# Image loads in fp32 through SyncE with casts on ScalarE, in a 3x3 convolution bound by its transfers

## Chip, cores, metric

One core of one Trainium2 chip. The metric is device time of one execution in microseconds (us). Runs are called slow when they are over 1.5% above the fastest of the same kernel; ratios and verdicts use the other, fast runs alone. Spans and windows come from one profiled execution of each kernel, a fast one in every case here. In profile lines PE is TensorE, PEld its weight loads, DVE VectorE, ACT ScalarE, POOL GpSimd and SP SyncE; a q behind a name is the engine's instruction queue, which waits and issues transfers. HBM is the memory that x and the output lie in, PSUM the one that TensorE's sums lie in. A transfer has landed when its completion is signalled.

## The reference

A 3x3 convolution, padding 1, stride 1, fp32 in and out: x is 16 x 64 x 64 x 64, the weight 128 x 64 x 3 x 3, the output 16 x 128 x 64 x 64.

```python
x_pad = np.pad(x, ((0, 0), (0, 0), (1, 1), (1, 1)), mode='constant')
for b, co, ci, kh, kw in all_indices:      # five nested loops
    output[b, co] += weight[co, ci, kh, kw] * x_pad[b, ci, kh:kh+h, kw:kw+w]
```

16.8 MB are read and 33.6 MB written.

## The kernel before

Two images of 64 channels fill the 128 partitions, so the batch is worked off in eight pairs; below, "image p" is the 2.1 MB load of pair p. Two output rows are computed together from three groups of fp16 matmuls: U from the sums of two neighbouring image rows (`ss`), A and B from the image itself (`xs`). ScalarE copies U out of PSUM, VectorE adds it to A and B. Each pair has four blocks of 30 matmuls. Loads 1 to 7 are issued by GpSimd and cast to fp16 on the way (casting loads); image 0 comes in fp32 in four pieces and is cast by ScalarE.

```python
    xpool = ctx.enter_context(tc.tile_pool(name="xpool", bufs=5))
    opool = ctx.enter_context(tc.tile_pool(name="opool", bufs=8))
    ...
    x0 = opool.tile([128, H, W], F32, tag="ot", name="x0")
    cuts = [(0, 18), (18, 34), (34, 50), (50, 64)]
    for lo, hi in cuts:
        nc.sync.dma_start(x0[:, lo:hi, :], x_rows[0:128, lo:hi, :])
    ...
    def load(p):
        xs[p] = xpool.tile([128, H, W], F16, tag="xs", name="xs")
        keep(nc.gpsimd.dma_start(xs[p], x_rows[128 * p : 128 * p + 128, :, :]))

    for p in range(1, 5):
        load(p)
    ...
    for p in range(NP):
        if p + 1 < NP:
            for lo in (0, 16):
                sums(nc.gpsimd, p + 1, xs[p + 1], lo, 16)
        if p > 0 and p + 4 < NP:
            load(p + 4)
        ...
        for blk in range(4):
            ...
            U = group([(G1, None)])          # 6 matmuls
            ...                              # two copies of U by ScalarE
            A = group([(G21, 1), (G0, -1)])  # 12 matmuls, then two adds
            Bt = group([(G01, 0), (G2, 2)])  # 12 matmuls, then two adds
            if blk in parts:
                ...                          # stores of the pair by SyncE
```

Of the kernel before, what the change touches and what calls it, by code (L numbers as in the profile page):

```python
# [8 lines left out]
F32 = mybir.dt.float32  # L9
F16 = mybir.dt.float16  # L10


@with_exitstack
def kernel(
    ctx: ExitStack,
    tc: tile.TileContext,
    x: bass.AP,
    weight: bass.AP,
    out: bass.AP,
):  # L20
    nc = tc.nc
    B, CI, H, W = x.shape
    CO = weight.shape[0]
    assert H == 64 and W == 64 and CI == 64 and CO == 128 and B % 2 == 0
    NP = B // 2
    RB = 8

    keep = tc.keep_in_program_order
    x_rows = x.rearrange("b c h w -> (b c) h w")
    out_rows = out.rearrange("b co h w -> b co h w")  # L30
    w_flat = weight.rearrange("co ci kh kw -> co (ci kh kw)")

    const = ctx.enter_context(tc.tile_pool(name="const", bufs=1))
    psum = ctx.enter_context(tc.tile_pool(name="psum", bufs=8, space=bass.MemoryType.PSUM))
    xpool = ctx.enter_context(tc.tile_pool(name="xpool", bufs=5))
    opool = ctx.enter_context(tc.tile_pool(name="opool", bufs=8))
    spool = ctx.enter_context(tc.tile_pool(name="spool", bufs=3))
    upool = ctx.enter_context(tc.tile_pool(name="upool", bufs=4))


    w_raw = const.tile([CO, CI * 9], F32)
    nc.sync.dma_start(w_raw, w_flat)  # L42
    x0 = opool.tile([128, H, W], F32, tag="ot", name="x0")
    cuts = [(0, 18), (18, 34), (34, 50), (50, 64)]
    for lo, hi in cuts:
        nc.sync.dma_start(x0[:, lo:hi, :], x_rows[0:128, lo:hi, :])  # L46
    ident = const.tile([128, 128], F16)
    make_identity(nc, ident)
    w16 = const.tile([CO, CI * 9], F16)
    keep(nc.gpsimd.tensor_copy(w16, w_raw))  # L50

    xs = {0: xpool.tile([128, H, W], F16, tag="xs", name="xs")}

    def load(p):
        xs[p] = xpool.tile([128, H, W], F16, tag="xs", name="xs")
        keep(nc.gpsimd.dma_start(xs[p], x_rows[128 * p : 128 * p + 128, :, :]))  # L56

    for p in range(1, 5):
        load(p)


    ss = {}

    def sums(eng, p, src, lo, n):
        if p not in ss:
            ss[p] = spool.tile([128, H // 2, W], F16, tag="ss", name="ss")
        v = src.rearrange("p (j i) c -> p j i c", i=2)
        keep(
            eng.tensor_add(  # L69
                ss[p][:, lo : lo + n, :], v[:, lo : lo + n, 0, :], v[:, lo : lo + n, 1, :]  # L70
            )
        )


    Wt = const.tile([128, 5, 3, CO], F16)
    G0, G21, G1, G01, G2 = range(5)

    def wrow(i):
        return Wt[:, i, :, :].rearrange("p t c -> p (t c)")

    wps = {}
    for kh in (1, 2, 0):
        wp = psum.tile([128, 512], F32, tag="acc", name="wp")
        for k in range(3):
            t = 3 * kh + k
            for q in (0, 64):
                nc.tensor.matmul(wp[q : q + 64, k * CO : k * CO + CO], w16[:, t::9], ident)  # L87
        wps[kh] = wp[:, 0 : 3 * CO]
    keep(nc.scalar.copy(wrow(G1), wps[1]))  # L89
    sums(nc.vector, 0, x0, 0, RB)  # L90
    keep(nc.vector.tensor_sub(wrow(G21), wps[2], wrow(G1)))  # L91
    keep(nc.vector.tensor_sub(wrow(G01), wps[0], wrow(G1)))  # L92
    for n, (lo, hi) in enumerate(cuts):
        keep(nc.scalar.copy(xs[0][:, lo:hi, :], x0[:, lo:hi, :]))  # L94
        if n == 0:
            keep(nc.scalar.copy(wrow(G0), wps[0]))  # L96
            keep(nc.scalar.copy(wrow(G2), wps[2]))  # L97
        if n < 3:
            sums(nc.vector, 0, x0, RB * (n + 1), RB)

    for p in range(NP):
        if p + 1 < NP:
            for lo in (0, 16):
                sums(nc.gpsimd, p + 1, xs[p + 1], lo, 16)
        if p > 0 and p + 4 < NP:
            load(p + 4)
        ots = [
            opool.tile([128, H // 2, 2, W], F32, tag="ot", name="ot") for _ in range(2)
        ]
        for blk in range(4):  # L110
            j0 = blk * RB

            def group(wi_rows):

                tiles = [
                    psum.tile([128, RB, W], F32, tag="acc", name="acc") for _ in range(2)
                ]
                n = 3 * len(wi_rows)
                i = 0
                for wi, off in wi_rows:  # L120
                    for kw in (1, 0, 2):
                        c_lo, c_hi = max(0, 1 - kw), min(W, W + 1 - kw)
                        for b2 in range(2):
                            p0 = 64 * b2
                            lo, hi = j0, j0 + RB
                            if off is None:
                                rhs = ss[p][p0 : p0 + 64, lo:hi, c_lo + kw - 1 : c_hi + kw - 1]
                            else:
                                while 2 * lo + off < 0:
                                    lo += 1  # L130
                                while 2 * (hi - 1) + off > H - 1:
                                    hi -= 1
                                first = 2 * lo + off
                                last = 2 * (hi - 1) + off
                                rhs = xs[p][
                                    p0 : p0 + 64,
                                    first : last + 1 : 2,
                                    c_lo + kw - 1 : c_hi + kw - 1,
                                ]
                            nc.tensor.matmul(  # L140
                                tiles[b2][:, lo - j0 : hi - j0, c_lo:c_hi],
                                Wt[p0 : p0 + 64, wi, kw, :],
                                rhs,
                                start=i == 0,
                                stop=i == n - 1,
                            )
                        i += 1
                return tiles

            U = group([(G1, None)])  # L150
            us = []
            for b2 in range(2):
                ut = upool.tile([128, RB, W], F32, tag="ut", name="ut")
                keep(nc.scalar.copy(ut, U[b2]))  # L154
                us.append(ut)
            A = group([(G21, 1), (G0, -1)])
            for b2 in range(2):
                nc.vector.tensor_add(ots[b2][:, j0 : j0 + RB, 0, :], A[b2], us[b2])  # L158
            Bt = group([(G01, 0), (G2, 2)])
            for b2 in range(2):  # L160
                nc.vector.tensor_add(ots[b2][:, j0 : j0 + RB, 1, :], Bt[b2], us[b2])  # L161
            parts = {3: (0, 64)} if p < NP - 1 else {1: (0, 32), 3: (32, 64)}
            if blk in parts:
                lo, hi = parts[blk]
                for b2 in range(2):
                    nc.sync.dma_start(
                        out_rows[2 * p + b2, :, lo:hi, :],
                        ots[b2].rearrange("p j i c -> p (j i) c")[:, lo:hi, :],
                    )


# [28 lines left out]
```

## Time and profile before

| | before |
|---|---|
| time, first runs (the last counts as slow) | 127.51, 128.91, 129.74 us |
| span of the profiled run | 125.7 us |
| busy: PE, VectorE, ScalarE, GpSimd | 107.0, 83.7, 40.8, 34.8 us |
| HBM traffic | 50.6 MB |

Busy time has to be read against what ends the kernel. The prediction quotes the rows that show both TensorE and the DMA engines full. What decides between them is the end of the chain of waits (columns: start, length, what), and whom SyncE, which issues the stores, waited for (total us, times, longest):

```profile
112.55 0.68 DVE ot L158
113.22 0.60 DVE ot L161
113.82 0.60 DVEq L195
```

```profile
SPq L166 <- DVE ot L161: 101.7, 17, 21.2
SPq L195 <- DMA out_dram<-ot: 8.9, 4, 2.4
```

The chain ends with VectorE 11 us before the span does. The closing lines of SyncE (L195) then wait 8.9 us for stores.

These are the groups that the change touches (busy us, mean ns of one; idle before it and its releaser):

```profile
L69 POOL TENSOR_TENSOR ss<-xs 128x1024 f16<-128x1024 f16 x14 | 29.5, 2125 | 23.1 <-DMA xs<-in_x_dram 9.3
L56 POOL DMA_DIRECT2D xs<-in_x_dram x7 | 4.0, 575 | 15.8 <-PE acc L140 15.8
```

### The profile page before, as it was taken

To read this page: it belongs to the slowest core of one execution; us is meant where nothing else is said; L and a number is where in the kernel's file an instruction comes from. 1 tells how busy PE (TensorE), PEld (TensorE's weight loads), DVE (VectorE), ACT (ScalarE), POOL (GpSimd) and SP (SyncE) were. 2 spreads that over 40 slices of the span, in tenths; PEclk is the share of its full clock that TensorE was granted. 3 is DMA by queue.
4 is the path that set the end of the run, shared out by engine and by line. 5 is a ranking of instruction groups with operands and counts; after the bars stand their busy time and mean duration, and the time that the engine had idled before them with its cause. 6 is when DMAs were issued, how large, how long until landed. Compare 5 with 4: busy or idle time off the path is not lost.

```text
span 125.7 us, 2408 instructions
## 1 busy us (share of the span) xinstructions
PE 107.0 (85%) x978; PEld 55.9 (44%) x978; DVE 83.7 (67%) x134; ACT 40.8 (32%) x72; POOL 34.8 (28%) x28
## 2 busy tenths in 40 slices
PE   0489799999999999999999999999999999990000
PEld 0334355555555555555555555555555555540000
DVE  0180798778877777877787778777877787773000
ACT  4283833333333333324333333333333333330000
POOL 2710297893029201930930093000000000000000
PEclk9999999999999999999999999999999999999755
DMA  4999999999999999999999999999999999999980
GB/s 130 325 353 216 224 214 222 211 182 331 326 305 362 315 315 323 422 321 326 307 409 443 433 427 438 417 422 433 427 433 438 417 422 433 427 417 422 422 370 34
DMA packets 4330, 43.43 MB, mean 345 GB/s; under 512 B 480, under 2 KB 480, under 8 KB 1120
## 3 DMA queue, kind: packets, MB, share of 16 engines
q1 hardware_dynamic: 3312, 35.95, 68.5%
q0 software_dynamic: 1008, 7.34, 28.5%
q8 instruction: 7, 0.11, 0.3%
q14 instruction: 3, 0.02, 0.0%
HBM read 17.07 MB, written 33.55 MB: 403 GB/s over the span
## 4 chain that ended last, share of the span: by engine, by line
PE 77%; DMA 8%; ACT 2%; SPq 1%; DVE 1%; issue 1%; DVEq 0%
PE acc L140 77%; DMA x<-in_x_dram 8%; SPq L46 1%; ACT ut L154 1%; ACT xs L94 1%; DVE ot L158 1%; DVEq L195 0%; DVE ot L161 0%; SPq L42 0%; DVEq L158 0%
## 5 line engine op out<-in xcount | busy, mean ns | idle before, releaser
L140 PE MATMUL acc<-xs,Wt 64*128 64x504 f16 (+3 forms) x768 | 95.1, 379 | 0.8 <-ACT ut L154 0.7
L140 PEld LDWEIGHTS <-Wt 64*128 64x128 f16 x960 | 54.8, 96 | 52.4 <-issue 5.1
L158 DVE TENSOR_TENSOR ot<-acc,ut 128x512 f32<-128x512 f32 x64 | 41.2, 686 | 21.2 <-PE acc L140 18.0
L154 ACT COPY ut<-acc 128x512 f32<-128x512 f32 x64 | 34.2, 589 | 64.1 <-issue 59.6
L161 DVE TENSOR_TENSOR ot<-acc,ut 128x512 f32<-128x512 f32 x64 | 41.1, 685 | 0.0
L69 POOL TENSOR_TENSOR ss<-xs 128x1024 f16<-128x1024 f16 x14 | 29.5, 2125 | 23.1 <-DMA xs<-in_x_dram 9.3
L140 PE MATMUL acc<-ss,Wt 64*128 64x504 f16 (+1 forms) x192 | 32.5, 384 | 0.9 <-DVE ss L69 0.9
L69 DVE TENSOR_TENSOR ss<-x 128x512 f16<-128x512 f32 x4 | 2.8, 690 | 9.6 <-DMA x<-in_x_dram 9.6
L56 POOL DMA_DIRECT2D xs<-in_x_dram x7 | 4.0, 575 | 15.8 <-PE acc L140 15.8
L87 PE MATMUL wp<-ident,w 128*64 128x128 f16 x18 | 1.3, 328 | 4.5 <-POOL w L50 4.5
L94 ACT CAST xs<-x 128x1024 f16<-128x1024 f32 (+2 forms) x4 | 4.1, 1052 | 2.4 <-DMA x<-in_x_dram 2.4
L87 PEld LDWEIGHTS <-w 128*64 128x64 f16 x18 | 1.1, 209 | 4.5 <-POOL w L50 4.5
L89 ACT ACT_TABLE_LOAD x1 | 1.3, 1283 | 0.7 <-PEq L184 0.7
L89 ACT CAST Wt<-wp 128x384 f16<-128x384 f32 x1 | 0.5, 480 | 3.1 <-PE wp L87 3.1
L50 POOL CAST w<-w_raw 128x576 f16<-128x576 f32 x1 | 0.7, 662 | 2.5 <-DMA w_raw<-in_weight_dram 2.5
L96 ACT CAST Wt<-wp 128x384 f16<-128x384 f32 x1 | 0.5, 479 | 0.5 <-DVE Wt L92 0.5
L91 DVE TENSOR_TENSOR Wt<-wp,Wt 128x384 f16<-128x384 f32 x1 | 0.6, 550 | 0.0
L92 DVE TENSOR_TENSOR Wt<-wp,Wt 128x384 f16<-128x384 f32 x1 | 0.5, 548 | 0.0
L97 ACT CAST Wt<-wp 128x384 f16<-128x384 f32 x1 | 0.5, 485 | 0.0
masks.py:199 POOL TENSOR_SCALAR_AFFINE_SELECT ident<-ident 128x128 f16<-128x128 f16 x1 | 0.3, 292 | 0.1
masks.py:197 POOL MEMSET ident<- 128x128 f16 x1 | 0.2, 204 | 0.3 <-POOLq L184 0.3
L184 POOL MEMSET const-float32-0.0<- 128x1 f32 x1 | 0.1, 98 | 0.2 <-issue 0.2
(3 smaller groups left out, 0.3 us busy)
## 6 DMA issues: line engine op xcount, KB each, us to landing
out_dram<-ot SPq DMA_DIRECT2D x14, 2048.0 KB, 18.1
xs<-in_x_dram POOLq DMA_DIRECT2D x7, 1024.0 KB, 15.4
out_dram<-ot SPq DMA_DIRECT2D x4, 1024.0 KB, 10.2
x<-in_x_dram SPq DMA_DIRECT2D x2, 512.0 KB, 6.0
x<-in_x_dram SPq DMA_DIRECT2D x1, 576.0 KB, 4.7
x<-in_x_dram SPq DMA_DIRECT2D x1, 448.0 KB, 9.9
w_raw<-in_weight_dram SPq DMA_DIRECT2D x1, 288.0 KB, 3.0
```

Source lines behind the costliest of these rows:

```text
L46: nc.sync.dma_start(x0[:, lo:hi, :], x_rows[0:128, lo:hi, :])
L50: keep(nc.gpsimd.tensor_copy(w16, w_raw))
L56: keep(nc.gpsimd.dma_start(xs[p], x_rows[128 * p : 128 * p + 128, :, :]))
L69: eng.tensor_add(ss[p][:, lo : lo + n, :], v[:, lo : lo + n, 0, :], v[:, lo : lo + n, 1, :])
L87: nc.tensor.matmul(wp[q : q + 64, k * CO : k * CO + CO], w16[:, t::9], ident)
L89: keep(nc.scalar.copy(wrow(G1), wps[1]))
L91: keep(nc.vector.tensor_sub(wrow(G21), wps[2], wrow(G1)))
L94: keep(nc.scalar.copy(xs[0][:, lo:hi, :], x0[:, lo:hi, :]))
L140: nc.tensor.matmul(tiles[b2][:, lo - j0 : hi - j0, c_lo:c_hi], Wt[p0 : p0 + 64, wi, kw, :], rhs, start=i == 0, stop=i == n - 1,)
L154: keep(nc.scalar.copy(ut, U[b2]))
L158: nc.vector.tensor_add(ots[b2][:, j0 : j0 + RB, 0, :], A[b2], us[b2])
L161: nc.vector.tensor_add(ots[b2][:, j0 : j0 + RB, 1, :], Bt[b2], us[b2])
```

## The change

The intent: take descriptor work and casting away from GpSimd's DMA path. All loads become fp32 on SyncE's hardware queue, into three staging buffers (where an fp32 image waits for its cast); ScalarE, half idle, casts them to fp16; the row sums read the fp32 buffers. To make room, `xs` shrinks from five buffers to three and the output from eight to six. The weight cast moves to VectorE.

```diff
-    xpool = ctx.enter_context(tc.tile_pool(name="xpool", bufs=5))
-    opool = ctx.enter_context(tc.tile_pool(name="opool", bufs=8))
+    xpool = ctx.enter_context(tc.tile_pool(name="xpool", bufs=3))
+    stage = ctx.enter_context(tc.tile_pool(name="stage", bufs=3))
+    opool = ctx.enter_context(tc.tile_pool(name="opool", bufs=6))
...
+    def load(p):
+        xf[p] = stage.tile([128, H, W], F32, tag="xf", name="xf")
+        for lo, hi in cuts if p == 0 else [(0, H)]:
+            keep(nc.sync.dma_start(
+                xf[p][:, lo:hi, :], x_rows[128 * p : 128 * p + 128, lo:hi, :]))
+
+    def cast(p, n):
+        if p not in xs:
+            xs[p] = xpool.tile([128, H, W], F16, tag="xs", name="xs")
+        lo, hi = cuts[n]
+        keep(nc.scalar.copy(xs[p][:, lo:hi, :], xf[p][:, lo:hi, :]))
+
+    for p in range(4):
+        load(p)
...
-                sums(nc.gpsimd, p + 1, xs[p + 1], lo, 16)
-        if p > 0 and p + 4 < NP:
-            load(p + 4)
+                sums(nc.gpsimd, p + 1, xf[p + 1], lo, 16)
...                                         # in each block, after the copies of U:
+            if p == 0 and blk < 3:
+                cast(0, blk + 1)
+            if p + 1 < NP:
+                cast(p + 1, blk)
...                                         # after the adds, before the stores:
+            if blk == 3 and p + 4 < NP:
+                load(p + 4)
```

More of the change, by code (lines that the diff above doesn't have):

```diff
@@ L42 @@
     nc.sync.dma_start(w_raw, w_flat)
-    x0 = opool.tile([128, H, W], F32, tag="ot", name="x0")
     cuts = [(0, 18), (18, 34), (34, 50), (50, 64)]
-    for lo, hi in cuts:
-        nc.sync.dma_start(x0[:, lo:hi, :], x_rows[0:128, lo:hi, :])
+    xf, xs = {}, {}
+    def load(p):
+        xf[p] = stage.tile([128, H, W], F32, tag="xf", name="xf")
+        for lo, hi in cuts if p == 0 else [(0, H)]:
+            keep(
+                nc.sync.dma_start(
+                    xf[p][:, lo:hi, :], x_rows[128 * p : 128 * p + 128, lo:hi, :]
+                )
+            )
+    def cast(p, n):
[5 more added lines that the diff above has]
+        load(p)
     ident = const.tile([128, 128], F16)
@@ L49 @@
     w16 = const.tile([CO, CI * 9], F16)
-    keep(nc.gpsimd.tensor_copy(w16, w_raw))
-    xs = {0: xpool.tile([128, H, W], F16, tag="xs", name="xs")}
-    def load(p):
-        xs[p] = xpool.tile([128, H, W], F16, tag="xs", name="xs")
-        keep(nc.gpsimd.dma_start(xs[p], x_rows[128 * p : 128 * p + 128, :, :]))
-    for p in range(1, 5):
-        load(p)
+    keep(nc.vector.tensor_copy(w16, w_raw))
     ss = {}
@@ L89 @@
     keep(nc.scalar.copy(wrow(G1), wps[1]))
-    sums(nc.vector, 0, x0, 0, RB)
+    sums(nc.vector, 0, xf[0], 0, RB)
     keep(nc.vector.tensor_sub(wrow(G21), wps[2], wrow(G1)))
     keep(nc.vector.tensor_sub(wrow(G01), wps[0], wrow(G1)))
-    for n, (lo, hi) in enumerate(cuts):
-        keep(nc.scalar.copy(xs[0][:, lo:hi, :], x0[:, lo:hi, :]))
-        if n == 0:
-            keep(nc.scalar.copy(wrow(G0), wps[0]))
-            keep(nc.scalar.copy(wrow(G2), wps[2]))
-        if n < 3:
-            sums(nc.vector, 0, x0, RB * (n + 1), RB)
+    cast(0, 0)
+    keep(nc.scalar.copy(wrow(G0), wps[0]))
+    keep(nc.scalar.copy(wrow(G2), wps[2]))
+    for n in range(1, 4):
+        sums(nc.vector, 0, xf[0], RB * n, RB)
     for p in range(NP):
@@ L165 @@
                 for b2 in range(2):
-                    nc.sync.dma_start(
+                    keep(nc.sync.dma_start(
                         out_rows[2 * p + b2, :, lo:hi, :],
                         ots[b2].rearrange("p j i c -> p (j i) c")[:, lo:hi, :],
-                    )
+                    ))
 _INS = ['x', 'weight']
```

## The prediction

> **What bounds the kernel now.** I read the page first (engines, slices, queues, chain), then the windows, then the list of waits, of SyncE too. The page points at TensorE:
>
> ```profile
> PE 107.0 (85%) x978; PEld 55.9 (44%) x978; DVE 83.7 (67%) x134; ACT 40.8 (32%) x72; POOL 34.8 (28%) x28
> PE   0489799999999999999999999999999999990000
> DMA  4999999999999999999999999999999999999980
> PE 77%; DMA 8%; ACT 2%; SPq 1%; DVE 1%; issue 1%; DVEq 0%
> ```
>
> Two rows are full, PE and DMA, and the chain credits 77% to PE. But that chain breaks off at 113.82 us with the last adds, while the span is 125.7 us. What follows is read in the windows (columns: window, its length, busy us of PE, PEld, DVE, ACT, POOL, then granted clock, DMA share, GB/s):
>
> ```profile
> 2.00:5.00 3.00, 0.50 (x8) 0.50 (x10) 0.00 (x0) 0.02 (x1) 1.21 (x2) 1.00 0.97 292
> 16.00:26.00 10.00, 10.00 (x98) 5.28 (x96) 8.43 (x15) 3.22 (x6) 8.66 (x6) 1.00 1.03 214
> 78.00:110.00 32.00, 32.00 (x303) 16.88 (x300) 24.99 (x41) 10.74 (x20) 0.00 (x0) 1.00 1.00 427
> 114.00:121.00 7.00, 0.00 (x0) 0.00 (x0) 0.42 (x1) 0.00 (x0) 0.00 (x0) 0.77 1.01 426
> 121.00:125.70 4.70, 0.00 (x0) 0.00 (x0) 0.00 (x0) 0.00 (x0) 0.00 (x0) 0.50 0.31 131
> ```
>
> PE is silent after about 113 us, yet the DMA engines work at 426 GB/s until 121. They hold a backlog of output:
>
> ```profile
> out_dram<-ot SPq DMA_DIRECT2D x14, 2048.0 KB, 18.1
> HBM read 17.07 MB, written 33.55 MB: 403 GB/s over the span
> ```
>
> A 2 MB store takes 2.1 MB / 427 GB/s = 4.9 us alone, but lands 18.1 us after its issue: three quarters of that is queueing. 50.62 MB at 427 GB/s are 118.5 us. So the kernel is bound by its transfers: first data near 1.75 us, DMA share about 1.0 throughout, last data near 122.8, then 2.9 us of completion and closing. I call an idle microsecond of the DMA engines a lost microsecond of the kernel; one of PE costs nothing until its slack is used up. The slack: the last half store is ready at about 114.5 us and would need only 4.9 us of transfer (to 119.4) against the 122.8 seen, so some 3 us.
>
> The GB/s count bytes written. In 16 to 26 us nearly all traffic is casting loads, 214 GB/s of fp16, which is 428 GB/s of fp32 read: the same rate as the pure stores.
>
> **What the skill says.** (1) "DMA: Bandwidth & Descriptors", section "Issuing engines are not separate DMA queues": DMAs from Sync, Scalar and GpSimd run on the same 16 engines and interleave; issuing from several saves only sequencer time. The trace agrees: share about 1.0 whether one queue or two have work. (2) Same page, "Where 436 GB/s comes from": the fabric ceiling is 435 GB/s. The 427 here is 98% of it, so fp32 loads cannot be clearly faster than the casting loads already are. (3) "ScalarE: Activation LUTs", "What ACT_TABLE_LOAD costs": an ACTIVATE with immediates takes 186 ns + 0.833 ns per element. For 1024 that is 1039 ns; the trace has 1058, and 1152 and 939 for 1152 and 896 elements. (4) "GPSIMD Engine Reference", "Elementwise — side-by-side cycle accounting": a two-input add is held at about 2.6 cycles per element by its read port. That is 2.2 us for 1024 elements at 1.2 GHz; the trace has 2125 ns for fp16. It speaks of cycles per element, not bytes, so I expect about 2.1 us from fp32 too, which no run here shows yet.
>
> **The change part by part.**
>
> Bytes. HBM traffic is the same 50.6 MB. Seven casting loads (14.7 MB read) become fp32 loads on the hardware queue. Their share was 28.5% of 125.7 us = 35.8 us, or 410 GB/s of source; at 427 the fp32 loads would take 34.4. I count the gain as 0 to 1 us. On the other side stands the only fp32 load traffic in the trace, the first window: 292 GB/s at share 0.97. Its rows are short (2.3 and 4.6 KB against 16 KB later) and it is the ramp, so I don't scale it to all loads, but it warns.
>
> ScalarE. 28 casts added beside the four there are: 7 x (1152 + 2 x 1058 + 939 ns) = 29.4 us, 40.8 to about 70 us busy. A block of 30 matmuls takes 3.24 us (copies start at 107.37 and 110.61); ACT spends 1.07 on its two copies and now 1.05 on a cast, 2.1 of 3.24. It fits, except in pair 0, where two casts make 3.2 of 3.24.
>
> GpSimd. Loses seven DMA issues (4.0 us) and the weight cast; its 14 adds stay at about 29.5 us. VectorE gains the weight cast, under 0.7 us. Neither is on the path.
>
> Start-up. The first four pieces of x no longer share the engines with casting loads: the last landed 9.9 us after issue, at 12.46. I estimate 8.7 us for its last data (1.46 MB left at 5 us, at about 400 GB/s). That relieves PE, which idled 0.7 us there.
>
> The hole. Staging has three buffers, so only images 0 to 2 are queued freely: 0.29 + 3 x 2.10 = 6.6 MB. Image 3 waits until staging buffer 0 is released by its last cast and sum, and SyncE cannot pass that load. Now step along ScalarE's order:
> - Image 1 has its last data at 8.7 + 2.10 MB / 427 GB/s = 13.6 us and lands near 14.0. In pair 0 ScalarE's first cast of image 1 stands in front of the copies of block 1 and of the later casts of image 0, so ScalarE waits for that landing.
> - From there: cast 1152 elements 1.15, two copies 1.07, cast 1.06, cast 1.06, two copies 1.07, cast 896 elements 0.94 = 6.35 us. Image 0's last cast ends near 20.3 us. VectorE's sums are long done.
> - Image 3 is issued then, and its data starts about 1.0 us later (weight issue at 0.74, data at 1.7), near 21.4.
> - Image 2's transfer ends at 13.6 + 4.9 = 18.5.
> The engines lie idle for about 2.9 us. The hole does not depend on when image 1 lands: both its edges move with it.
>
> After that. Image 4 needs casts of image 1 to end (about 23.5, while image 3 is moving until 26.3). Stores of pair 0 are ready near 25 and start at 31; from there the queue should stay ahead of the engines: image 5 at 36, stores of pair k ready at 24 + 13k us (4 blocks x 3.24 = 12.96). From 21.4 on remain five loads (10.5 MB) and 33.55 MB of stores, 44.0 MB: 103.1 us at 427 GB/s, ending at 124.5; with 0.5 us for the unevenness seen in the last window, 125.0. Plus 2.9 of closing: span 127.9, against 125.7. That is +2.2 us, or +1.8%. On the median of 128.91 it makes 131.1; I add 0.2 for the fp32 rate: 131.3 us.
>
> Output buffers: six instead of eight, three pairs. Pair 6 needs the stores of pair 3 landed, about 86.5 us, and first writes at about 91; pair 7: 96 against 104. A margin of over 4 us, so no new wait.
>
> **The rivals.**
> 1. Fp32 loads move slower than casting loads. For: the 292 GB/s start. Against: short rows and ramp there, stores of the same 16 KB rows at 427. If the seven loads ran at 360, they would take 40.8 us instead of 34.4: about 6 us more, over 135 us.
> 2. No hole, or one filled. If image 1's cast did not hold ScalarE, or traffic ran evener on one queue, the saturated time would stay or lose up to 1 us: 127.5 to 129. For: the casting queue is at 410, not 427. Against: buffer 0 has no other way to come free than this row of ScalarE work.
> 3. PE becomes the bound. ScalarE's wait delays pair 0: I put U of block 3 at about 20.2 us, as now (20.08). If it came 4 us later, the slack would be gone and each further us would show: 132 to 134. For: 3.2 of 3.24 us on ScalarE there. Against: PE gains at the start.
> 4. Faster, as a reader of the chain would say, since PE's start-up stall shrinks. That gain goes into the wait for the stores.
>
> **Range and chances.** The middle is +1.8%, just below the 2% line. Hole 2 to 4 us, rate from -1 to +2, PE stall 0 to 1.5; and the three runs before spread from 127.51 to 129.74. So 131.3 us, from 129.2 to 134.3. Faster 0.03, within 2% 0.52, slower 0.45.
>
> **What would show it.** Right: a DMA share near 0 for some 3 us between 18 and 22 us, and near 1.0 from there to about 122; PE done at 113 to 115; ScalarE near 70 us; GpSimd adds near 2.1 us; last data about 2 us later than now. Wrong: loads of 16 KB rows clearly under 410 GB/s (rival 1), no gap (rival 2), a PE gap in the middle (rival 3), or waits of VectorE's adds on landing stores (the output buffers).

## The result, and the profile after

| | before | after |
|---|---|---|
| time, median of the first runs | 128.9 us | 132.43 us (132.03 to 133.06) |
| ratio, first measurement | | 1.0315, 95% interval 1.022 to 1.041 |
| ratio, second measurement with more rounds | | 1.0402, 1.037 to 1.043 |
| span of the profiled run | 125.7 us | 130.2 us |

A ratio here is the mean time of one kernel's fast runs over that of the other's of the same rounds, so it is not quite the ratio of the medians. The median before is that of four runs, with the slow one. The kernel is slower by 3 to 4%.

The slices of the changed kernel (40 of them, 3.26 us each): DMA busy in tenths, and GB/s.

```profile
PE   0489979999999999999999999999999999800000
DMA  4999964999999999999999999999999999999970
GB/s 127 329 444 423 423 282 106 387 438 352 418 418 448 420 398 440 428 423 438 423 423 438 423 428 433 413 438 433 413 443 433 413 443 423 425 418 418 425 327 23
```

A notch stands in the DMA row, while PE has none worth the name. The notch is what the prediction calls the hole; below it is the gap. The windows around it (columns as in the prediction):

```profile
8.00:18.00 10.00, 9.07 (x66) 4.16 (x64) 6.05 (x10) 5.97 (x10) 3.34 (x2) 1.00 1.03 439
18.00:21.00 3.00, 3.00 (x32) 1.56 (x30) 2.47 (x5) 3.00 (x5) 2.85 (x2) 1.00 0.14 55
21.00:24.00 3.00, 3.00 (x32) 1.64 (x30) 2.27 (x5) 2.20 (x4) 3.00 (x2) 1.00 0.86 262
30.00:33.00 3.00, 3.00 (x32) 1.56 (x29) 2.27 (x5) 2.02 (x3) 3.00 (x2) 1.00 0.94 322
40.00:110.00 70.00, 70.00 (x660) 37.13 (x656) 54.37 (x88) 41.47 (x63) 14.08 (x6) 1.00 1.01 428
```

Three things are to be seen. Whole fp32 images (8 to 18 us) move at 439 GB/s, no slower than stores (428), so the loads themselves are not the cost. (The DMA share of 1.03 in that line shows that a window counts packets whole where they start; at a share of 1.00 it would be 426 GB/s.) From 18 to 24 us, 0.95 MB move where 427 GB/s would have moved 2.56 MB: 1.61 MB or 3.8 us are missing. In windows of 0.2 us the bulk of image 2 ends at 18.4 us and the next data starts at 21.4, so 3.0 us of the 3.8 are empty and 0.8 a slow restart (an estimate, as are all such differences here). And from 30 to 33 us, where loads give way to the first stores, another (427 - 322) x 3 / 427 = 0.7 us are missing. Together 4.5 us, and the span is 4.5 us longer. That the two agree to a tenth is partly chance, since other stages differ too: from 115 us to the end the changed kernel lacks 4.0 us of transfer at 427 GB/s, the kernel before 3.3.

The packet records in the kept traces (a packet here is 16 KB of fp32 of one partition) show what the 1.5 us outside the empty time are. A packet takes 611 ns in the median. In the changed kernel 64 packets take over 700 ns, up to 1.75 us, 50 of them at 21 to 23 us and at 30 to 33 us; their time above 611 ns is 0.74 us of all 16 DMA engines at the restart and 0.60 at the changeover. So the engines had work there and did it slowly. In `four_staging` below, 19 packets are as slow, 0.42 us in the whole run. A casting packet of the kernel before, which reads 16 KB and writes 8, takes 624 ns: fp32 loads are quicker by some 2%.

Why the engines had nothing to do is read from ScalarE's timeline (start, length, line, what, count, and in brackets the idle time before it and its releaser) and from SyncE's waits:

```profile
14.61 1.15 ACT L60 CAST xs<-xf 128x1152 f16<-128x1152 f32 x1 [4.03 <-DMA xf<-in_x_dram]
15.67 1.07 ACT L158 COPY ut<-acc 128x512 f32<-128x512 f32 x2
16.63 2.00 ACT L60 CAST xs<-xf 128x1024 f16<-128x1024 f32 x2
18.52 1.08 ACT L158 COPY ut<-acc 128x512 f32<-128x512 f32 x2
19.48 1.91 ACT L60 CAST xs<-xf 128x896 f16<-128x896 f32 x2
```

```profile
SPq L51 <- ACT xs L60: 43.4, 5, 10.5
```

ScalarE stands still for 4.03 us until image 1 has landed, then works through the row that the prediction counted. Image 0's last cast is the first of the two at 19.48; it ends at 20.4. Only then may SyncE issue image 3 into staging buffer 0. (Most of the 43.4 us of waiting at L51 costs nothing: later loads wait while stores queue.)

The groups concerned:

```profile
L77 POOL TENSOR_TENSOR ss<-xf 128x1024 f16<-128x1024 f32 x14 | 32.9, 2370 | 50.5 <-DMA xf<-in_x_dram 50.5
L60 ACT CAST xs<-xf 128x1024 f16<-128x1024 f32 (+2 forms) x32 | 33.7, 1060 | 4.8 <-DMA xf<-in_x_dram 4.8
```

The casts cost what was expected, off the path. GpSimd's adds became slower (2370 ns from fp32 against 2125 from fp16), off the path too.

### The profile page after: what moved, and what is told of

It reads as the page before. It is cut to its first block, busy times and chain, and to the rows that moved or that the text cites. A ratio compares the mean times of both kernels' runs of the same rounds, so it can differ in the third digit from the quotient of the medians.

```text
span 130.2 us, 2437 instructions
## 1 busy us (share of the span) xinstructions
PE 106.8 (82%) x978; PEld 56.3 (43%) x978; DVE 84.4 (65%) x135; ACT 67.0 (51%) x100; POOL 33.6 (26%) x20
## 4 chain that ended last, share of the span: by engine, by line
PE 80%; DMA 4%; DVE 2%; ACT 1%; issue 1%; DVEq 0%; SPq 0%
PE acc L144 80%; DMA xf<-in_x_dram 4%; ACT xs L60 1%; DVE ot L166 1%; DVE ss L77 1%; DVE ot L169 0%; DVEq L205 0%; ACT ut L158 0%; SPq L43 0%; DVEq L166 0%
## 5 line engine op out<-in xcount | busy, mean ns | idle before, releaser
L144 PE MATMUL acc<-xs,Wt 64*128 64x504 f16 (+3 forms) x768 | 89.6, 380 | 0.9 <-ACT xs L60 0.9
L77 POOL TENSOR_TENSOR ss<-xf 128x1024 f16<-128x1024 f32 x14 | 32.9, 2370 | 50.5 <-DMA xf<-in_x_dram 50.5
L60 ACT CAST xs<-xf 128x1024 f16<-128x1024 f32 (+2 forms) x32 | 33.7, 1060 | 4.8 <-DMA xf<-in_x_dram 4.8
L144 PE MATMUL acc<-ss,Wt 64*128 64x504 f16 (+1 forms) x192 | 27.1, 384 | 1.4 <-DVE ss L77 1.4
L77 DVE TENSOR_TENSOR ss<-xf 128x512 f16<-128x512 f32 x4 | 2.8, 690 | 2.7 <-DMA xf<-in_x_dram 2.7
L67 DVE CAST w<-w_raw 128x576 f16<-128x576 f32 x1 | 0.5, 460 | 3.7 <-DMA w_raw<-in_weight_dram 3.7
```

Of the source, the lines that this page charges most:

```text
L60: keep(nc.scalar.copy(xs[p][:, lo:hi, :], xf[p][:, lo:hi, :]))
L67: keep(nc.vector.tensor_copy(w16, w_raw))
L77: eng.tensor_add(ss[p][:, lo : lo + n, :], v[:, lo : lo + n, 0, :], v[:, lo : lo + n, 1, :])
L144: nc.tensor.matmul(tiles[b2][:, lo - j0 : hi - j0, c_lo:c_hi], Wt[p0 : p0 + 64, wi, kw, :], rhs, start=i == 0, stop=i == n - 1,)
```

## The experiments

Theory: the DMA engines bound the kernel, and the loss is the gap, because image 3 waits for staging buffer 0, which hangs on ScalarE's order. Rivals: fp32 loads are slower than casting loads; TensorE is the bound; the number of buffers costs by itself.

All ten runs below were made beside the kernel before. The MB column is worked out from windows (GB/s times length, summed) and gives what had been moved by 40 us; the lag divides the shortfall against `four_staging` (its two profiles: 15.70 and 15.72, mean 15.71 MB) by 427 GB/s. The last column is the median less the 127.96 us of `four_staging`.

| kernel | median us | ratio to before (95%) | MB by 40 us | lag us | time beyond four_staging, us |
|---|---|---|---|---|---|
| after (first, again) | 132.43, 132.46 | 1.0315; 1.0402 | 13.94, 13.98 | 4.2, 4.0 | 4.5, 4.5 |
| later_image3 | 136.60 | 1.0705 (1.065 to 1.076) | 11.94 | 8.8 | 8.6 |
| fewer_matmuls | 131.81 | 1.0323 (1.025 to 1.040) | 13.89 | 4.3 | 3.8 |
| casts_first | 129.74 | 1.0172 (1.009 to 1.026) | 14.96 | 1.7 | 1.8 |
| image1_in_pieces | 129.84 | 1.0203 (1.015 to 1.025) | 15.09 | 1.4 | 1.9 |
| four_staging (first, again) | 127.96, 127.97 | 1.0044; 1.0028 | 15.70, 15.72 | 0 | 0 |
| staging4_casts_first | 127.87 | 0.9984 (0.996 to 1.001) | 15.85 | -0.3 | -0.1 |
| staging4_two_pieces | 127.79 | 0.9975 (0.995 to 1.000) | 15.82 | -0.3 | -0.2 |

The runs were made in three calls, each on another chip, so medians of different calls are compared with some caution. Within the second call, on one chip, `changed_again` took 132.46 us and `four_staging_again` 127.97. The verdicts on record are "slower" for the change, "same" for `four_staging_again`, `four_staging_whole0` and both kernels named staging4, and "unclear" for the others; the intervals of `later_image3` and `changed_again` lie wholly above 1.02 all the same.

What a kernel has failed to move by 40 us it lacks at the end, nearly one for one. The one kernel left out of the table, `four_staging_whole0`, starves its transfers later too and is told below.

### casts_first

```diff
     for n in range(1, 4):
+        cast(0, n)
         sums(nc.vector, 0, xf[0], RB * n, RB)
...
-            if p == 0 and blk < 3:
-                cast(0, blk + 1)
```

> The changed kernel with one thing moved: the three later casts of image 0 stand ahead of pair 0, in front of the first cast of image 1, so staging buffer 0 comes free near 12 to 13 us instead of 20.4. Hole theory (the 3.5 us lost are the time the DMA engines wait for image 3's load to be issued): the gap between 18.4 and 21.3 us goes; image 3 follows image 2 without a break; only a short gap of about 0.5 to 1 us may open near 23.4 us, when image 4 still waits for buffer 1; span 126 to 127 us instead of 130.2, ratio to the kernel before 0.98 to 1.00. Slow-load theory (fp32 loads on the hardware queue move slower than casting loads): the time stays at 130 us or more.

Measured: 129.74 us, span 127.5. The notch at 18 us is gone. A smaller one opened at the expected place, and a second loss behind it:

```profile
18.00:23.00 5.00, 5.00 (x50) 2.62 (x48) 4.76 (x9) 3.77 (x6) 4.83 (x3) 1.00 0.99 419
23.00:25.00 2.00, 2.00 (x22) 1.10 (x20) 1.39 (x3) 1.51 (x3) 1.48 (x1) 1.00 0.90 262
27.00:30.00 3.00, 3.00 (x31) 1.60 (x28) 2.27 (x5) 1.78 (x4) 3.00 (x2) 1.00 1.02 279
```

At 23 to 25 us image 4 comes late, since it waits for buffer 1, whose last cast ends at 22.2: (427 - 262) x 2 / 427 = 0.8 us, of which only some 0.25 are empty time and the rest slow packets. At 27 to 30, where stores take over, 1.0 us more. So moving one wait took away over half of the loss and uncovered the next wait of the same kind; the expected 0.98 to 1.00 was missed by that second loss, which the expectation did not have.

### four_staging

```diff
-    stage = ctx.enter_context(tc.tile_pool(name="stage", bufs=3))
+    stage = ctx.enter_context(tc.tile_pool(name="stage", bufs=4))
...
-    spool = ctx.enter_context(tc.tile_pool(name="spool", bufs=3))
+    spool = ctx.enter_context(tc.tile_pool(name="spool", bufs=2))
```

> The changed kernel with four staging buffers instead of three (paid for with two buffers of row sums instead of three); ScalarE's order is left as it is. Hole theory: image 3 is queued at the start with no wait, image 4 is issued when buffer 0 comes free near 20.4 us while image 3 moves until 23.4; no gap at all; span 125 to 126.5 us, ratio 0.98 to 0.995. If ScalarE's wait for image 1 itself (and not the buffer) were the cost, the time would stay near 130 us, since ScalarE still waits for it and PE is as late.

Measured: 127.96 us, ratio 1.0044; again, with more rounds:

> Four staging buffers once more with more rounds: the same as the kernel before within 1% (transfer theory: same bytes, same rate, no gap); if fp32 loads on the hardware queue were slower than casting loads by the 1 us that the interval of the first run still allows, the ratio would be 1.008 or more.

127.97 us, 1.0028 (1.000 to 1.005).

```profile
18.00:24.00 6.00, 5.79 (x56) 3.09 (x57) 4.75 (x9) 5.68 (x9) 4.09 (x2) 1.00 1.02 429
24.00:40.00 16.00, 16.00 (x154) 8.55 (x152) 12.63 (x21) 10.20 (x15) 7.08 (x4) 1.00 1.00 422
100.00:104.00 4.00, 4.00 (x42) 2.19 (x40) 3.42 (x6) 1.52 (x3) 0.00 (x0) 1.00 0.92 389
```

No gap, and no loss where the stores take over. ScalarE still waits 4.51 us for image 1 in this kernel (4.03 in the changed one), and TensorE is as late; so it is the buffer and not ScalarE's standstill that costs. With the gap closed nothing of the slowdown is left to give to slower fp32 loads, beyond 0.3% (0.5% at the end of the interval). The last line shows the limit of this version: the store of pair 6 is ready only at 102 us, and for some 0.4 us the engines run short. Output buffers are six here as well, so their number costs nothing that these runs resolve.

### later_image3

```diff
         xf[p] = stage.tile([128, H, W], F32, tag="xf", name="xf")
+        if p == 3:
+            keep(nc.vector.memset(xf[p][:, 0, 0:1], 0.0))
...
-    for p in range(4):
+    for p in range(3):
         load(p)
...
+            if blk == 3 and p == 0:
+                load(3)
```

> The changed kernel with image 3's load held back further: a one-element write into its staging buffer by VectorE after the last adds of pair 0 makes the load wait for them, near 24.5 us instead of 20.4. Hole theory: the gap grows by about 4 us and the time with it by the same 4 us, one for one: span near 134 us, 136 to 137 us measured. PE theory (the kernel is bound by TensorE as the chain of waits has it): image 3 is needed only from 37 us on, so no matmul waits and the time stays within 0.5 us of the changed kernel.

Measured: 136.60 us, 4.2 us above the changed kernel; the span is 134.7 us, 4.5 above. TensorE still finishes early (last adds at 115.7 us).

```profile
18.00:26.00 8.00, 8.00 (x79) 4.34 (x76) 6.16 (x12) 6.83 (x11) 5.91 (x3) 1.00 0.08 27
26.00:30.00 4.00, 4.00 (x41) 2.07 (x37) 3.27 (x7) 2.40 (x4) 0.00 (x0) 1.00 0.94 340
34.00:40.00 6.00, 6.00 (x61) 3.22 (x57) 4.68 (x8) 3.94 (x6) 4.37 (x3) 1.00 0.99 366
```

Image 3's data starts at 25.9 us instead of 21.4, so the gap is 4.5 us longer. PE is full throughout it and no matmul waits for image 3, yet the time follows the gap one for one. The restart again costs 0.8 us ((427 - 340) x 4 / 427), and the changeover to stores 0.9 us. The PE theory falls.

One wait here is new, and it is the one that the prediction named as the sign of too few output buffers: at 93.6 us VectorE's adds, and with them TensorE, waited for a store to land.

```profile
PE acc L146 <- DVE ot L168: 1.6, 1, 1.6
```

TensorE's slack took it up. But the predicted margin of "over 4 us" is used up by a delay of this size.

### fewer_matmuls

```diff
-                n = 3 * len(wi_rows)
+                n = 2 * len(wi_rows)
-                    for kw in (1, 0, 2):
+                    for kw in (1, 0):
```

> The changed kernel with one of three column taps left out of all convolution matmuls, a third of TensorE's work (wrong result on purpose). Transfer theory: PE busy falls to about 70 us and its row shows gaps, but the bytes are the same and the hole hangs on ScalarE and transfers; the time stays within 1% of the changed kernel's 132.4 us. PE theory (77 to 80% of the chain is PE): the time falls by 20 us or more.

Wrong on purpose. Measured: 131.81 us, ratio 1.0323, span 129.4 us.

```profile
PE 83.2 (64%) x658; PEld 40.6 (31%) x658; DVE 82.1 (63%) x135; ACT 67.1 (52%) x100; POOL 33.5 (26%) x20
PE   0499359999999979941999269951999970000000
DMA  4999965899999999999999999999999999999981
```

A third of the convolution matmuls is gone, PE's row is full of gaps, the DMA row is as before, and the time fell by 0.6 us. (Busy PE fell to 83 and not to 70 us. In part this is the granted clock: it was 0.50 at 19 to 21 us, and only 8 matmuls fall into each of these microseconds, where the changed kernel has 12 to 14 at 1.00.) The changed kernel's page credits its chain of waits to the engines like this:

```profile
PE 80%; DMA 4%; DVE 2%; ACT 1%; issue 1%; DVEq 0%; SPq 0%
```

These 80% say nothing on what a faster PE would be worth.

### image1_in_pieces

```diff
-        for lo, hi in cuts if p == 0 else [(0, H)]:
+        for lo, hi in cuts if p < 2 else [(0, H)]:
```

> The changed kernel, three staging buffers and ScalarE's order kept, with image 1 loaded in the same four pieces as image 0. ScalarE's first cast of image 1 then waits for a piece that lands near 10.5 us and not for the whole image at 14.6. Hole theory with the chain of the prediction: ScalarE's wait of 4.0 us all but goes, buffer 0 comes free near 16.5 us instead of 20.4, image 3 is issued before image 2 ends at 18.4, no gap; span near 126 us, ratio 0.99 to 1.01. If it were the three buffers as such, whatever ScalarE waits for, the gap would stay and the time with it (ratio 1.03).

Measured: 129.84 us, ratio 1.0203.

```profile
11.04 1.15 ACT L60 CAST xs<-xf 128x1152 f16<-128x1152 f32 x1 [0.57 <-DMA xf<-in_x_dram]
16.50 1.90 ACT L60 CAST xs<-xf 128x896 f16<-128x896 f32 x2
```

```profile
19.00:20.00 1.00, 1.00 (x12) 0.51 (x10) 0.38 (x1) 1.00 (x3) 0.00 (x0) 1.00 0.63 164
27.00:30.00 3.00, 3.00 (x30) 1.50 (x28) 2.27 (x5) 1.78 (x4) 3.00 (x2) 1.00 0.98 289
```

ScalarE's wait for image 1 is 0.57 us, image 0's last cast ends at 17.4 instead of 20.4 (16.5 had been expected), and the loss there shrinks to 0.6 us, most of it slow packets. This ties the gap to ScalarE's wait with three buffers kept. The loss did not go wholly: 17.4 plus about 1 us to first data falls on the time at which image 2 ends. Behind it follows the loss at the changeover again (1.0 us at 27 to 30). A little over half of the loss is gone rather than all: the chain was right, the expected size was not.

### changed_again

The changed kernel itself.

> The changed kernel once more, beside the others on the same chip: 132 to 133 us, ratio 1.03, an empty stretch of 2.9 us and a slow restart of about 1 us behind it. It sets the scale for the two others of this call.

132.46 us, ratio 1.0402 (1.037 to 1.043), with the same gap (0.21 MB in 19 to 22 us) and the same losses behind it.

### four_staging_whole0

`four_staging` with image 0 in one load:

```diff
-        for lo, hi in cuts if p == 0 else [(0, H)]:
+        for lo, hi in [(0, H)]:
```

> Four staging buffers, and image 0 as one load with 16 KB rows instead of four pieces with rows of 3.6 to 4.6 KB. If short rows cost rate at the start (about 290 GB/s from 2 to 5 us and 380 from 5 to 8, against 430 later), some 0.5 to 1 us of transfer is saved, and the kernel is the fastest so far if TensorE's later start (near 9.5 us instead of 6.9) stays inside its slack of some 2 us; if the slow start is only a start-up, the rates stay and the time is the same or up to 1 us longer.

Measured: 129.20 us, ratio 1.011 (1.006 to 1.016).

```profile
2.00:5.00 3.00, 0.76 (x14) 0.76 (x14) 0.46 (x1) 0.13 (x2) 0.00 (x0) 1.00 0.98 356
5.00:8.00 3.00, 0.56 (x10) 0.47 (x9) 0.00 (x0) 0.38 (x1) 0.00 (x0) 1.00 1.02 437
23.00:24.00 1.00, 1.00 (x13) 0.52 (x10) 0.46 (x1) 1.00 (x3) 1.00 (x1) 1.00 0.65 147
```

Against 279 and 374 GB/s in the same windows of `four_staging`, the start did become faster, so one long load moves quicker than four short ones. The gain was lost again: ScalarE and TensorE begin later (first cast at 8.92 us), buffer 0 comes free later, and image 4 arrives late at 22 to 24 us.

### staging4_casts_first and staging4_two_pieces

The two measures together, then with image 0 in two pieces so that TensorE starts early and most of it moves in long rows:

```diff
-        for lo, hi in cuts if p == 0 else [(0, H)]:
+        for lo, hi in [(0, 18), (18, H)] if p == 0 else [(0, H)]:
```

> Four staging buffers and image 0's casts ahead of pair 0. No gap, as with four staging buffers alone; in addition TensorE loses its stall of about 1 us in pair 0, so the store of pair 6 is ready 1 us earlier than in four_staging, whose transfers dip to 389 GB/s at 100 to 104 us. Transfer theory: at most 0.4 us better than four_staging: ratio to the kernel before 0.995 to 1.003.

> The same with image 0 in two pieces, rows 0 to 18 (4.6 KB a row of the transfer) and 18 to 64 (11.8 KB), so that TensorE starts as early as now and most of image 0 moves in long rows. If long rows are what made four_staging_whole0 move 0.35 to 0.4 MB more by 18 us, this gains 0.3 to 0.6 us on staging4_casts_first: ratio 0.990 to 1.000, the fastest of all; if the early rate is only a start-up, it equals staging4_casts_first.

Measured: 127.87 us, 0.9984; and 127.79 us, 0.9975 (0.995 to 1.000). No gap in either, and the dip at 100 to 104 us is gone or smaller (422 and 410 GB/s against 389). From 5 to 8 us the two pieces move 412 GB/s against 382 of the four, but the times differ by less than their spread, so the second step is not shown to gain. Both are level with the kernel before in its fast runs; neither beats it by a margin that counts. Their spread differs, though: their 22 runs each lie between 127.6 and 128.4 us, while 22 of 43 runs of the kernel before in the same rounds were slow, up to 135.2, with no break between fast and slow; the median of all 43 is 129.14 us. No slow run was profiled, so nothing is said here of the cause.

## Why the prediction came out as it did

The time (132.43 us) lies in the stated range and the direction is right. But the middle, +1.8%, was too small against 3.2 and 4.0%, and the largest chance, 0.52, went to "within 2%". By its own steps:

- Bound by transfers, with 3 us of slack for TensorE: right. Shown by `fewer_matmuls` (a third of the matmuls for 0.6 us) and `later_image3` (a longer gap, one for one).
- Bytes and rate: right. An fp32 packet takes 611 ns, a casting one 624; rival 1 is out. The 292 GB/s of the start were no sign of slow fp32 loads.
- ScalarE: right. 28 casts of about 1.06 us, absorbed outside pair 0; 67.0 us busy where about 70 had been predicted.
- GpSimd's adds at 2.1 us from fp32: wrong, 2.37 us. It did not matter.
- The hole, "about 2.9 us": right nearly to the digit. Image 1 usable at 14.6 (14.0 predicted), last cast of image 0 at 20.4 (20.3), bulk of image 2 over at 18.4 (18.5), next data at 21.4 (21.4). That it fits to a tenth is luck: image 1 was usable 0.6 us later than predicted, and the row of ScalarE's work behind it took 5.8 us instead of 6.35, since neighbouring instructions overlap in the timeline. The two errors cancel. Nor did both edges of the hole move with image 1, as the prediction says: image 2 ended no later. The hole as such is shown as the cause by `four_staging`, `casts_first` and `image1_in_pieces`, each of which lets the buffer come free earlier, or does without it, in another way.
- "44.0 MB: 103.1 us at 427 GB/s" after the hole: this term failed. It takes the transfers to be at full rate from the first byte. Measured are 0.8 us of slow restart (21 to 24 us) and 0.7 us at the first changeover from loads to stores (30 to 33 us). The prediction had the restart before its eyes: it quotes 292 GB/s for the kernel's start, and used it for a doubt on the rate of all loads, not for the price of a second start. With these 1.5 us its +2.2 becomes +3.7; the spans differ by 4.5. Of the remaining 0.8 us some 0.6 lie in the end: the prediction allowed 2.9 + 0.5 us there, and 4.0 us of transfer are missing after 115 us.
- Output buffers: no wait, as said. Rival 3 (a later TensorE): block 3 of pair 0 began at 20.32 us, 20.2 predicted; no cost.

Open: why packets are slow at a restart and at the changeover to stores, which loses 0.7 to 1.0 us. The changed kernel, `casts_first`, `image1_in_pieces` and `later_image3` show it, all with a gap or a late load before; `four_staging`, without one, does not. The packet records show that packets take longer there, not why; nothing here tests a reason.

## What to carry to other kernels

When two resources look full, look at what still works after the other has stopped, and cut the suspect's work: a chain of waits may give 80% to an engine whose speed is worth next to nothing. In a kernel bound by transfers, count the time in which the queue has nothing it may start: ring buffers that are released by an in-order engine make a load wait for whatever that engine waits for, and a gap cost its length plus a restart here (3.0 and 0.8 us). A buffer more, a reordered release and a finer load each treat the same gap; after each, look for the next wait of the same kind.

## What the Trainium skill lacked or had wrong

- "DMA: Bandwidth & Descriptors", "Where 436 GB/s comes from", says without a condition that for transfers between HBM and SBUF the HBM side at about 358 GB/s binds, and in the same paragraph calls its own measurement of 425 GB/s near the fabric's rate. With one core running, the first does not hold here: stores sustained 427 to 428 GB/s, and fp32 loads were no slower (611 ns for a packet of 16 KB).
- No page of those consulted gives the price of a pause in a saturated queue: here 0.8 us of lost transfer at the restart, and 0.7 to 1.0 us at the next changeover from loads to stores, beyond the pause itself.
- No page of those consulted compares a casting load with a plain one: here 624 ns against 611 for 16 KB read.
- "GPSIMD Engine Reference", "Elementwise — side-by-side cycle accounting", measures its add in fp32 alone (4497 ns for 2048 elements) and gives one count of cycles per element for it. Here an add of 1024 elements took 2370 ns from fp32 and 2125 ns from fp16, 12% more.
